# TensorE's instructions tied to the program's order in three stages of an encoder layer, and six more filling steps ahead of the attention's scores

## The chip, the cores and the metric

The kernel runs on one NeuronCore of one Trainium2 chip. The metric is the device time of one execution in microseconds. A core has engines with one in-order instruction stream each: TensorE (PE: matrix products, and transposes as products with an identity; PEld is its loading of the stationary operand), VectorE (DVE), ScalarE (ACT), GpSimd (POOL) and SyncE (SP, which issues most DMAs here). They meet at semaphores.

## What is computed

One layer on a sequence of 1024 tokens of width 1024, all in float32:

```
x = x + 1/2 post1(SwiGLU1(pre1(x)))                       # FFN, 2816 wide
u = pre_mix(x)
q,k,v,g of the retention | q,k,v of the attention | two gates = u @ W_mix_in
y_ret = W_ret_out(silu(g) * headnorm(retention forward + backward))   # 4 heads, chunks of 128
y_na  = W_na_out(neighbourhood attention on a 16 x 64 grid, 8 heads of 64, 8 x 16 window, with a bias)
x = x + post_mix(W_mix_out(sigmoid(gate_ret) * y_ret + sigmoid(gate_na) * y_na))
x = x + 1/2 post2(SwiGLU2(pre2(x)))
```

pre and post are RMS norms.

## The kernel before

**Products.** float32 is carried as a high part and a low part (`Core.split`: ScalarE casts the high part at L60, VectorE subtracts at L61). `Core.mm3` (L85 to L89) makes one product of three TensorE instructions: high by high (L87), high by low (L88), low by high (L89). The big products of the FFNs and of W_mix_in use a Strassen-Winograd scheme (`Winograd`, `Pairs`). PSUM has eight banks: six go round under the name `ps`, two under `pt` (transposes).

**Who sets the order.** The program is traced in the order in which Python emits it, and at the end a planner orders each engine's instructions. It simulates the engines with costs of its own and gives an engine, among the instructions whose inputs are ready in that simulation, the one that was emitted first. So an instruction that isn't ready in the plan is overtaken by later ones that are. The chip then runs each engine's stream strictly in the planned order. It is the planner, too, that hands out the buffers of a tile's name.

**The attention** (`na_cores`, called at L1262). 32 units: 4 pairs of heads, 8 units each. A unit's steps:

- scores (`scores`, L744): two heads, two products of 384 columns each; VectorE adds the bias and finds the maximum (L745), ScalarE takes exp (L749), VectorE the reciprocal (L751) and the scaling (L753). The tile `s` has two buffers.
- `flip` (L763): six transposes into two `pt` banks, split to `pth` and `ptl` by ScalarE and VectorE (L60, L61).
- `values`: nine products of 256 columns, copied to `ot` by ScalarE (L779).

The loop emits, for i: the scores of unit i, `fill(n1)`, the flip of unit i-1, the values of unit i-2, `fill(n2)`. Ahead of the loop it loads the first keys and queries and calls `fill(n0)`. The three numbers are `NA_FILL`.

**Filling.** `Filler` steps a generator, `products` (L1227 on): the retention's v (two projections of 64 steps, the lines of `vproj`, L1121; their banks are copied out at L1139), then the two sigmoid gates (`gate`, L1221 and L1223, 192 steps), then W_na_out (64 steps, L1254 and L1256). A step is one `mm3` of 512 columns. One more step only sets the mark "rv". After the attention, `fill.until("rv")` makes sure that v is done.

**The retention** (`ret_cores`, called at L1266). Four heads of eight chunks: backwards, states from `update` (L922) with `fill` between; then per chunk scores (L936), three products (L1010 to L1013), norms on ScalarE, VectorE and GpSimd (L949 to L957), and `store` with two transposes (L966). `RET_FILL` holds its counts of filling steps. What is left of the generator runs in `fill.drain()` behind it. Then W_ret_out (L1294) reads the result back and splits it into `xy`.

**From W_mix_out's product to the last norm** (L1331 on). `Core.out_proj` works on groups of token tiles (0,1,2), (3,4,5), (6,7), two banks for each tile. `Ep` takes the finished banks of a tile through the post norm (squares L219, scaling L226 that frees the banks, residual L228, squares L230) and `norm_T` through FFN2's pre norm (L117). Its transposes (`Core.flip`, L126) are kept in the list `left` for some products and emitted between them. `Winograd.put` makes FFN2's operands of them. `Pairs.lead` then makes the first two products of four pairs of FFN2, with the last tiles' transposes emitted between; FFN2 (`ffn_in`) follows.

Of the kernel before, what the change touches and what calls it, by code (L numbers as in the profile page):

```python
# [1 line left out]

# [1 line left out]

# [22 lines left out]
RH = 4  # L27
NHP = 4

NA_FILL = (12, 2, 2)  # L30
RET_FILL = (14, 2, 2, 4, 2, 3, 0, 1, 2)
FLIP_FILL = (8, 8, 8, 8, 2)
NA_UNITS = ((0, 0, 0), (3, 1, 0), (1, 0, 1), (1, 0, 2), (4, 1, 1), (4, 1, 2), (2, 0, 3), (5, 1, 3))
# [4 lines left out]
class Core:  # L38
# [97 lines left out]
    def out_proj(self, nk, lhs, wload, done, groups=((0, 1, 2), (3, 4, 5), (6, 7)), tail=3, lag=8, space=3):  # L136

        left = []  # L140

        def one(t, k, a, w):
            for e in [e for e in left if e[0] <= 0]:
                left.remove(e)
                f = e[1]()
                if f is not None:
                    left.append([2, f])
            for b in range(2):
                self.mm3(banks[t][b], a[t], w[b], k == 0, k == nk - 1)
            for e in left:  # L150
                e[0] -= 1

        for toks in groups:
            banks = {t: [self.bank() for _ in range(2)] for t in toks}
            tl = tail if len(toks) > 1 else 0
            for k in range(nk - tl):
                w, a = wload(k), lhs(k, toks)
                for t in toks:
                    one(t, k, a, w)
            last = [(k, lhs(k, toks), wload(k)) for k in range(nk - tl, nk)]  # L160
            for t in toks:
                for k, a, w in last:
                    one(t, k, a, w)
                f = done(t, banks[t])
                if f is not None:
                    left.append([max(lag, max([e[0] for e in left], default=-space) + space), f])
        return [f for _, f in left]


class Filler:  # L170
# [267 lines left out]
class LeftFactors:  # L438


    order = [j + h * FT // 2 for j in range(FT // 2) for h in range(2)]
# [232 lines left out]
def stream(c, pool, src):  # L674

    def lhs(k, toks):
        n = len(toks) * P
        p0 = toks[0] * P
        raw = pool.tile([P, 384], F32, tag="graw", name="graw", bufs=2)
        h = pool.tile([P, 384], F32R, tag="gh", name="gh", bufs=3)  # L680
        l = pool.tile([P, 384], F32R, tag="gl", name="gl", bufs=3)
        c.nc.sync.dma_start(raw[:, :n], src(k)[:, p0:p0 + n])
        c.split(h[:, :n], l[:, :n], raw[:, :n])
        return {t: (h[:, j * P:(j + 1) * P], l[:, j * P:(j + 1) * P]) for j, t in enumerate(toks)}
    return lhs
# [344 lines left out]
def trunk_layer(ctx: ExitStack, tc, x, g1a, w1i, w1o, g1b, gma, wmt, wnv, wrv, logits, dtab, rope, bias,  # L1030
# [7 lines left out]
    c = Core(tc, const, wpool, psum, dram)  # L1038
# [18 lines left out]
    def rows(a):  # L1057
        return lambda t: a[t * P:(t + 1) * P, :]
# [3 lines left out]
    def pool(stack, name, side="left"):  # L1062
        return stack.enter_context(tc.tile_pool(name=name, bufs=1, side=side))
# [28 lines left out]
    ep = pool(ep_stack, "ep1")  # L1092
# [165 lines left out]

    fill = Filler(products())
    dec = []  # L1260
    with tc.tile_pool(name="na", bufs=1) as na:
        na_cores(c, na, d, bias, fill, *NA_FILL, {24: lambda: dec.append(Decays(c, mix, logits, dtab))})  # L1262
    dec = dec[0]
    fill.until("rv")
    with tc.tile_pool(name="ret", bufs=1) as ret:
        ret_cores(c, ret, mix, d, dec, fill, RET_FILL)  # L1266
    y_stack = ExitStack()
    ypool = pool(y_stack, "y")
# [44 lines left out]
    cmb = pool(left, "cmb2")  # L1313
    wx = Winograd(c, (apool,) * 3, cmb, (14,) * 7)
    wx.s3_on_pool = (4, 5)
    with tc.tile_pool(name="ep2", bufs=1) as ep:
        rest = c.out_proj(KT, stream(c, gs, lambda k: d["m"][k]), lambda k: c.load_w(wmo[k]),
                          Ep(c, ep, gmb, g2a, False, rows(x1), rows(x2), wx.put))
        fin = Pairs(c, wx, [(w2i[i], w2i[FT + i]) for i in LeftFactors.order], 3, 1)

        def save():
            return [gs.tile([P, 384], F32, tag=n, name=n, bufs=3)[:, :256] for n in ("gh", "gl")]

        fin.lead(save, rest)
        for f in rest:
            f()
# [94 lines left out]
```

## Time and profile before

| | us |
|---|---|
| median of 3 runs | 2334.3 (2330.53 to 2337.57) |
| the profiled execution | 2332.5 |
| its span, first to last instruction | 2330.7 |
| TensorE busy | 2226.6 (96%) |
| VectorE busy | 1677.0 (72%) |
| ScalarE busy | 1008.0 (43%) |
| GpSimd busy | 598.9 (26%) |

In the chain that ended last TensorE has 84% of the span. The attention takes from about 998 to 1246 us, the retention to 1471, W_ret_out to about 1558, W_mix_out's product and its norms to 1706. In the rows, `out<-in` are the program's tile names, a number behind "L" is a line of the kernel, and "idle before" is the time in which the engine stood still before the instruction, with what ended it. A product's rows overlap: the distance of two starts is what the product costs in a row of them.

### The profile page before, as it was taken

Reading aid. Unit: us, or ns where it says so; the run is one execution under the profiler, and the core shown is the slowest. Engines: PE = TensorE matmul, PEld = TensorE weight load, DVE = VectorE, ACT = ScalarE, POOL = GpSimd, SP = SyncE. Lnnn points to the kernel's source line nnn. Section 1 sums busy time; section 2 is a strip of 40 time slices with the busy share of each in tenths; the row PEclk is TensorE's granted clock in tenths of the full one; section 3 lists DMA queues with packets and bytes.
Section 4 is the critical chain, followed back from the end, with each engine's and each line's share of the span. In section 5 each row is a group of like instructions: output and inputs, shape, how many; then the busy total and the mean of one; then the engine's idle time right before and its main releaser. Section 6 shows DMA issues by size and latency. Waiting matters only on the chain.

```text
span 2330.7 us, 30323 instructions
## 1 busy us (share of the span) xinstructions
PE 2226.6 (96%) x10288; PEld 1849.4 (79%) x10288; DVE 1677.0 (72%) x2939; ACT 1008.0 (43%) x2104; POOL 598.9 (26%) x749
## 2 busy tenths in 40 slices
PE   6999999999998999989889999998889999999998
PEld 5888888778886888877768888887668888887886
DVE  7887777745878588867865678545887778775575
ACT  6332222344553223367765676324633222234453
POOL 3144343300440144311101222101322434431032
PEclk9999999999998999999989999999999999999999
DMA  5355555576753444466634467765524555547674
GB/s 190 109 181 174 197 177 185 199 233 189 257 175 112 168 131 131 137 217 202 195 107 152 161 222 231 263 230 188 194 91 142 197 176 200 181 154 235 190 243 142
DMA packets 161884, 422.64 MB, mean 181 GB/s; under 512 B 19712, under 2 KB 47488, under 8 KB 161664
## 3 DMA queue, kind: packets, MB, share of 16 engines
q1 hardware_dynamic: 121248, 286.97, 38.4%
q0 software_dynamic: 40480, 133.72, 15.6%
q8 instruction: 81, 1.33, 0.2%
q14 instruction: 75, 0.61, 0.1%
HBM read 301.60 MB, written 123.21 MB: 182 GB/s over the span
## 4 chain that ended last, share of the span: by engine, by line
PE 84%; issue 6%; DVE 4%; DMA 2%; ACT 2%; POOL 1%; SPq 0%; POOLq 0%; DVEq 0%; ACTq 0%
PE ps L87 26%; PE ps L88 26%; PE ps L89 26%; PE pt L88 1%; PE pt L89 1%; PE pt L87 1%; DMA graw<-g0a 1%; PE pt L126 1%; DVE tmp L117 0%; DVE wl L61 0%; DMA graw<-m 0%; PE pt L914 0%; DMA kraw<-nk 0%; PE pt L966 0%; DVE gl L61 0%
## 5 line engine op out<-in xcount | busy, mean ns | idle before, releaser
L61 DVE TENSOR_TENSOR wl<-wraw,wh 128x512 fp32r<-128x512 f32 x662 | 460.3, 719 | 97.4 <-ACT wh L60 94.5
L60 ACT CAST wh<-wraw 128x512 fp32r<-128x512 f32 x670 | 391.7, 619 | 277.3 <-PE ps L88 110.0
L87 PE MATMUL ps<-wh,gh 128*128 128x512 f32 x612 | 239.2, 393 | 17.2 <-ACT gh L60 12.8
L88 PE MATMUL ps<-wl,gh 128*128 128x512 f32 x612 | 239.4, 391 | 0.0
L61 DVE TENSOR_TENSOR gl<-graw,gh 128x512 fp32r<-128x512 f32 (+2 forms) x178 | 128.9, 728 | 149.2 <-ACT gh L60 146.0
L89 PE MATMUL ps<-wh,gl 128*128 128x512 f32 x612 | 229.1, 392 | 1.1 <-DVE gl L61 1.1
L60 ACT CAST gh<-graw 128x512 fp32r<-128x512 f32 (+2 forms) x178 | 106.5, 602 | 210.6 <-PE ps L88 72.0
L87 PEld LDWEIGHTS ps<-wh,gh 128*128 128x128 f32 x612 | 115.5, 189 | 44.8 <-ACT gh L60 12.9
L526 POOL TENSOR_TENSOR q<-q,gain 128x512 f32<-128x512 f32 x30 | 58.1, 1958 | 334.4 <-PE ps L88 122.1
L89 PEld LDWEIGHTS ps<-wh,gl 128*128 128x128 f32 x612 | 114.8, 188 | 26.3 <-DVE gl L61 2.8
L88 PEld LDWEIGHTS ps<-wl,gh 128*128 128x128 f32 x612 | 115.5, 189 | 23.7
L60 ACT CAST wh<-t 128x512 fp32r<-128x512 f32 x58 | 36.1, 623 | 192.7 <-DVE t L384 192.6
L87 PE MATMUL ps<-a11h,wh 128*128 128x512 f32 x280 | 113.1, 404 | 1.9 <-DVE tmp L226 1.9
L89 PE MATMUL ps<-a11h,wl 128*128 128x512 f32 x280 | 111.7, 399 | 0.0
L88 PE MATMUL ps<-a11l,wh 128*128 128x512 f32 x280 | 111.4, 398 | 0.0
L87 PE MATMUL ps<-a12h,wh 128*128 128x512 f32 x280 | 110.6, 395 | 0.1
L88 PE MATMUL ps<-a12l,wh 128*128 128x512 f32 x280 | 109.8, 392 | 0.0
L89 PE MATMUL ps<-a12h,wl 128*128 128x512 f32 x280 | 109.6, 391 | 0.0
L87 PE MATMUL ps<-a22h,wh 128*128 128x512 f32 x280 | 109.5, 391 | 0.0
L89 PE MATMUL ps<-a22h,wl 128*128 128x512 f32 x280 | 109.2, 390 | 0.0
L88 PE MATMUL ps<-a22l,wh 128*128 128x512 f32 x280 | 109.1, 389 | 0.0
L400 DVE TENSOR_TENSOR c<-ps,gt 128x512 f32<-128x512 f32 x44 | 30.4, 691 | 107.2 <-PE ps L89 107.1
(362 smaller groups left out, 6006.6 us busy)
## 6 DMA issues: line engine op xcount, KB each, us to landing
wraw<-in_dram SPq DMA_DIRECT2D x243, 512.0 KB, 4.3
lead<-in_dram POOLq DMA_DIRECT2D x44, 256.0 KB, 3.9
g0s<-cmb POOLq DMA_DIRECT2D x44, 256.0 KB, 3.2
graw<-g0s SPq DMA_DIRECT2D x44, 256.0 KB, 2.8
wq<-in_dram POOLq DMA_DIRECT2D x44, 256.0 KB, 3.8
g1s<-cmb POOLq DMA_DIRECT2D x44, 256.0 KB, 2.7
graw<-g1s SPq DMA_DIRECT2D x44, 256.0 KB, 2.7
bt<-in_dram SPq DMA_DIRECT2D x24, 384.0 KB, 3.9
```

Of the source, the lines that this page charges most:

```text
L60: nc.scalar.copy(h, src)
L61: (eng or nc.vector).tensor_tensor(l, src, hf, ALU.subtract)
L87: mm(ps, a[0], b[0], start=start, stop=False, skip_group_check=more)
L88: mm(ps, a[0], b[1], start=False, stop=False, skip_group_check=more)
L89: mm(ps, a[1], b[0], start=False, stop=stop, skip_group_check=more)
L126: self.nc.tensor.transpose(pt[:, j * P:(j + 1) * P], h[:, j * P:(j + 1) * P], self.ident)
L400: self.last = self.read = tt(c21, p7, c12, ALU.add).ins
L526: (eng or c.nc.gpsimd).tensor_tensor(h if out is None else out, h, self.post[:, b * 512:(b + 1) * 512], ALU.mult)
```

## The change

Three `with` statements get a second manager, `in_order(c, mybir.EngineType.PE)`: around the attention, around the retention, and around the part from W_mix_out's product to the last norm and FFN2's first products. When such a block ends, every TensorE instruction traced in it gets an edge to the TensorE instruction traced before it. The edges are of the class `NoSync`: the planner keeps them, and no semaphore is added. Other engines are planned as before. `NA_FILL` goes from (12, 2, 2) to (18, 2, 2). No instruction is added or removed.

```diff
-NA_FILL = (12, 2, 2)
+NA_FILL = (18, 2, 2)
...
+@contextmanager
+def in_order(c, engine):
+
+    traced = c.nc.cur_bb.bb.instructions
+    n = len(traced)
+    yield
+    prev = None
+    for i in c.nc.cur_bb.bb.instructions[n:]:
+        if i.engine == engine:
+            if prev is not None:
+                c.tc.add_manual_dep(i, prev.name, mybir.DependencyInfo(
+                    mybir.DependencyClass.NoSync, mybir.DependencyReason.DATA), reason="order")
+            prev = i
...
-    with tc.tile_pool(name="na", bufs=1) as na:
+    with tc.tile_pool(name="na", bufs=1) as na, in_order(c, mybir.EngineType.PE):
         na_cores(c, na, d, bias, fill, *NA_FILL, {24: lambda: dec.append(Decays(c, mix, logits, dtab))})
...
-    with tc.tile_pool(name="ret", bufs=1) as ret:
+    with tc.tile_pool(name="ret", bufs=1) as ret, in_order(c, mybir.EngineType.PE):
         ret_cores(c, ret, mix, d, dec, fill, RET_FILL)
...
-    with tc.tile_pool(name="ep2", bufs=1) as ep:
+    with tc.tile_pool(name="ep2", bufs=1) as ep, in_order(c, mybir.EngineType.PE):
         rest = c.out_proj(KT, stream(c, gs, lambda k: d["m"][k]), lambda k: c.load_w(wmo[k]),
```

More of the change, by code (lines that the diff above doesn't have):

```diff
@@ L1 @@
-from contextlib import ExitStack
+from contextlib import ExitStack, contextmanager
 import numpy as np
```

## The prediction

> **What bounds the kernel now.** I read the table of busy time by stretch first (engines in the order PE, PEld, DVE, ACT, POOL; then the granted TensorE clock, the DMA share and GB/s).
>
> ```profile
> 998.00:1030.00 32.00, 25.50 (x107) 20.57 (x106) 21.79 (x50) 20.84 (x44) 5.23 (x7) 0.89 0.91 292
> 1030.00:1233.00 203.00, 180.64 (x980) 155.29 (x979) 142.44 (x423) 140.00 (x359) 15.17 (x21) 0.94 0.51 156
> 1233.00:1246.00 13.00, 9.75 (x47) 8.05 (x46) 4.64 (x8) 6.11 (x13) 1.07 (x2) 0.91 0.74 259
> 1246.00:1471.00 225.00, 224.27 (x1289) 195.53 (x1287) 163.90 (x426) 139.90 (x364) 53.87 (x84) 1.00 0.59 191
> 1585.00:1640.00 55.00, 48.70 (x215) 38.67 (x213) 38.34 (x69) 31.46 (x75) 7.07 (x11) 0.97 0.56 183
> 1640.00:1706.00 66.00, 49.62 (x217) 39.05 (x217) 59.32 (x98) 37.49 (x84) 24.00 (x25) 0.94 0.52 177
> ```
>
> The first three rows are the attention, the fourth the retention, the last two the stretch from W_mix_out's product to the last norm. TensorE is idle 6.5, 22.4 and 3.3 us in the attention, 0.7 in the retention, 6.3 and 16.4 behind W_mix_out. So the retention has nothing to win and something to lose, and the attention holds most of what the order can touch. In 1640 to 1706 VectorE is busy 59.32 of 66 us, TensorE 49.62: there the order of TensorE isn't the limit.
>
> Next, the waits of TensorE in the attention's long stretch, 1030 to 1233 (total, times, longest), and one of VectorE's:
>
> ```profile
> PE ps L87 <- ACT pth L60: 14.4, 10, 3.6
> PE ps L88 <- DVE ptl L61: 4.8, 4, 2.5
> PE pt L763 <- DVE ptl L61: 1.6, 3, 0.7
> ...
> DVE s L745 <- PE pt L763: 12.3, 9, 4.0
> ```
>
> 19.2 us of the 22.4 that TensorE is idle there are spent by the product with the values, which waits for the split of transposed probabilities (pth, ptl). The last row says that VectorE stands 12.3 us ahead of the scores' sum with the bias, because its tile s has two buffers and TensorE hasn't transposed the one before last. The timeline of TensorE (start, duration, instruction, idle time before it and who ended it) late in the attention:
>
> ```profile
> 1197.33 0.34 PE L744 MATMUL ps<-k,qh 128*128 128x384 f32 x1
> 1197.51 0.34 PE L744 MATMUL ps<-k,ql 128*128 128x384 f32 x1
> ...
> 1198.73 0.49 PE L763 MATMUL pt<-ident,s 128*128 128x128 f32 x3
> 1198.98 0.36 PE L88 MATMUL ps<-ptl,vh 128*128 128x256 f32 x1
> ...
> 1199.42 0.28 PE L88 MATMUL ps<-ptl,vh 128*128 128x256 f32 x1
> 1199.54 0.28 PE L89 MATMUL ps<-pth,vl 128*128 128x256 f32 x1
> 1202.63 0.54 PE L87 MATMUL ps<-pth,vh 128*128 128x256 f32 x1 [2.81 <-ACT pth L60]
> ...
> 1204.25 0.63 PE L87 MATMUL ps<-a21h,wh 128*128 128x512 f32 x1
> 1204.68 0.63 PE L88 MATMUL ps<-a21l,wh 128*128 128x512 f32 x1
> ...
> 1207.42 0.39 PE L88 MATMUL ps<-a21l,wh 128*128 128x512 f32 x1
> 1207.65 0.39 PE L89 MATMUL ps<-a21h,wl 128*128 128x512 f32 x1
> ```
>
> The planner has put the transposes late and close against the product with the values of the same unit; at 1202.63 the product stands 2.81 us for a split that began just before. The two filling products after it start 0.43 us apart, three microseconds later 0.23: after such a wait the clock is halved for a while. The program's own order puts a whole unit of other work between the two.
>
> **The change, part by part.** Durations are of the profiled execution (2332.5 us, 1.8 under the median of 2334.3).
>
> *The cycle in the order of emission.* Per unit: scores of unit i (4 products at 0.18, 1197.33 to 1197.51), two filling steps (6 at 0.23), six transposes of unit i-1 (some 0.1 each: three from 1198.73, 0.25 to the next product), nine products with the values of i-2 (at 0.12, 1199.42 to 1199.54), two filling steps: 0.7 + 1.4 + 0.6 + 1.1 + 1.4 = 5.2 us. From the transposes of a unit to its values lie 1.1 + 1.4 + 0.7 + 1.4 + 0.6 = 5.2 us of TensorE's work; the split there takes a few tile passes. So the **19.2 us are taken as gone**; bounds 0 and 19.2.
>
> *What is late next.* The transposes stand at the head of TensorE's queue, and behind them the values, the filling and the next scores. Between the scores of a unit and its transposes lie 1.4 + 0.6 + 1.1 + 1.4 + 0.7 + 1.4 = 6.6 us. The chain that has to fit (sum with the bias, exp, reciprocal, scaling) is seen in the timeline of the engines for two units:
>
> ```profile
> 1199.26 0.56 DVE L745 CUSTOM_DVE_ANT_0 s<-ps,bt 128x384 f32<-128x384 f32 x1 [0.98 <-PE pt L763]
> 1204.94 0.75 DVE L753 TENSOR_SCALAR s<-s,ss 128x384 f32<-128x384 f32 x2
> 1210.22 0.56 DVE L745 CUSTOM_DVE_ANT_0 s<-ps,bt 128x384 f32<-128x384 f32 x1 [1.02 <-PE pt L763]
> 1212.85 1.28 ACT L1223 ACT_TABLE_LOAD   x1
> 1217.59 0.75 DVE L753 TENSOR_SCALAR s<-s,ss 128x384 f32<-128x384 f32 x2
> ```
>
> 6.4 us (1199.26 to 1205.69) and 8.1 (1210.22 to 1218.34). Both begin only when the buffer of s is free; strict order transposes earlier, so that wait goes. At 6.4 the new stall is 0, at 8.1 it is 1.5 a unit, for some 31 units 47 us. The second holds a sigmoid between two table loads, which only the end of the stage has. I take 0.3 a unit, **+10**, near the lower end, because VectorE (142.44 of 203) and ScalarE (140.00) have slack.
>
> *The clock.* Granted 0.94 over 203 us is 12.2 us of full-speed work lost at most. Short waits don't cost it, as the quieter middle of the stage shows beside the 2.81 us wait:
>
> ```profile
> 1128.00:1188.00 60.00, 54.05 (x312) 46.30 (x311) 47.08 (x154) 44.49 (x120) 3.78 (x7) 1.00 0.63 196
> 1199.00:1207.00 8.00, 5.19 (x22) 4.43 (x20) 3.87 (x13) 5.66 (x14) 0.00 (x0) 0.79 0.09 35
> ```
>
> 6 us of idling in 60, and the clock stays at 1.00. With stalls of 0.3 a unit I take back **-8** (0 to -12.2). The Trainium skill (TensorE: Matmul & The Clock Gate, "The HAM clock gate") halves the clock only after an idle window of about 3.4 us. By that the wait of 2.81 would have cost nothing, and the trace disagrees: 0.43 us apart behind it. By the rule alone the term would be about -2, for the one wait of 3.6, and the sum 6 us higher.
>
> *Eighteen filling steps ahead of the scores.* 18 x 3 x 0.23 = 12.4 us from 998.46, to 1010.9; the first score product ran here at 1011.15.
>
> ```profile
> 998.46 0.39 PE L87 MATMUL ps<-wh,a11h 128*128 128x512 f32 x1
> ...
> 1011.15 0.34 PE L744 MATMUL ps<-k,qh 128*128 128x384 f32 x1
> ...
> 1017.45 0.44 PE L744 MATMUL ps<-k,qh 128*128 128x384 f32 x1 [1.03 <-DVE nast L745]
> ...
> 1023.01 1.66 PE L763 MATMUL pt<-ident,s 128*128 128x128 f32 x6 [4.40 <-DVE s L753]
> ```
>
> The old planner filled these microseconds without being told, so the six steps replace what it did: 0. The waits at 1017 and 1023 (5.4 us) are the first chain through an empty pipeline and stay. At the other end six steps are missing: 18 + 136 in the attention and 234 in the retention ask for 388 of the 385 that exist (384 of work and one that only marks), where 382 were asked for. In the last microseconds of the retention:
>
> ```profile
> 1467.92 0.51 ACT L957 ACTIVATE yn<-y,rstd 128x256 f32<-128x256 f32 x1 [0.94 <-POOL rstd L97]
> 1470.10 0.38 PE L966 MATMUL pt<-ident,yn 128*128 128x128 f32 x2
> 1470.57 2.94 ACT L60 CAST xy<-wraw 128x1024 fp32r<-128x1024 f32 x3 [2.14 <-PE pt L966]
> ```
>
> The last transposes could start at 1468.43 and start at 1470.10, behind filling; W_ret_out's first split waits for them. Taking 6 x 3 x 0.23 = 4.1 us of filling away lets this end 1.7 us sooner, so **+2.4** (0 to +4.1).
>
> *The change of stage.* The 3.3 us idle in 1233 to 1246 is the wait for the retention's first keys. In strict order 2 + 14 filling steps, 10.9 us, stand behind the last values; **-2** (0 to -3.3).
>
> *Retention in strict order.* Nothing can be gained beyond 0.7. Its cycle in the text of the program has four filling steps (2.7 us) in every chunk between a state's update and its use, and only the first updates stand close behind the transposes that feed them. I take **+3** (0 to +10).
>
> *From W_mix_out to the last norm.* Waits of TensorE in 1585 to 1714:
>
> ```profile
> PE ps L87 <- ACT s2h L60: 6.6, 1, 6.6
> PE ps L87 <- DVE tmp L226: 6.4, 4, 1.9
> PE ps L87 <- ACT gh L60: 5.4, 3, 3.0
> PE pt L126 <- DVE tmp L117: 3.9, 3, 2.2
> ```
>
> The L226 waits are for banks of the tiles before; in strict order the third token tile's first products block two others that now run ahead, which can double them (+6.4). At the end 48 products of FFN2's first factors stand behind the last transposes instead of ahead, 10.9 us that cover the 6.6 behind s2h, but they also delay by what they cover. VectorE's 59.32 of 66 us sets that end in either order: **0** (-8 to +10).
>
> Sum: -19.2 + 10 - 8 - 2 + 3 + 2.4 + 0 = -13.8. 2332.5 - 13.8 = 2318.7, and with the 1.8 to the median **2320.5 us**.
>
> **The rivals.** *The wait only changes its name* (0.25): the chain takes 7.2 us, 0.6 over what lies between, so 19 us of new stalls at the transposes instead of 10, and the clock returns 4 instead of 8: the sum is about -1, 2333. For it: VectorE waited 12.3 us for TensorE, and the planner, which put the transposes late, seems to reckon with a long chain. Against: the 12.3 us come from that lateness itself.
>
> *Slower* (0.18): the chain takes 8.1 us in every unit, as the one that ended at 1218.34. Then 47 us of stalls stand against 19.2, nothing comes back of the clock, and the sum is +31, 2366. It decides from 7.5 us on: 0.9 x 31 = 28, and -19.2 + 28 - 4 - 2 + 5.4 = +8. The Trainium skill's "A second HAM failure mode" on the same page points the same way: frequent small idling between groups of products can make the clock swing. Against it stands the row with 1.00 at 10% idle.
>
> *More* (0.12): the stalls stay near 0, the clock returns whole, and the covered end behind W_mix_out gives 8: -19.2 - 12.2 - 3.3 - 8 + 5.4 = -37, 2297.
>
> *It does nothing in the retention*: the planner's order there may already be the program's; that moves the sum by 3 and is inside the range.
>
> **How the numbers follow.** The forecast has 0.45. Its own range is 2308 to 2331. The range for 8 in 10 reaches down to the large gain and up past no change, not to the end of the slow case: 2298 to 2345. Within 0.3% is 2327.3 to 2341.3, what a measurement of this kernel can hardly tell from none. Faster: 0.43 of the forecast's 0.45, 0.12, and 0.02 of the first rival, 0.57. Same: 0.02, 0.20 and 0.02, 0.24. Slower: 0.03 and 0.16, 0.19.
>
> **What would show it.** Right: the waits for pth and ptl in the attention nearly gone, VectorE's wait for the transposes gone, the clock near 1.00 there, the attention some 17 us shorter, the retention within a few microseconds of 225. Wrong: a row of transposes waiting for s L753 of more than 20 us; a retention with idle TensorE; or banks (L226) holding the stretch behind W_mix_out for 10 us more than before.

## The result, and the profile after

| | us |
|---|---|
| median of 5 runs after | 2312.9 (2309.86 to 2314.31) |
| median of 5 runs before, same chip | 2334.7 (2330.53 to 2337.71) |
| ratio | 0.9904, 95% interval 0.9889 to 0.9919 |
| the profiled execution after | 2313.7 (span 2311.8) |

That is 21.8 us faster between the medians, where 13.8 were forecast. The table of busy time by stretch of the changed kernel (columns as in the prediction):

```profile
998.00:1030.00 32.00, 27.83 (x124) 22.16 (x123) 22.38 (x53) 22.48 (x49) 5.08 (x6) 0.95 0.89 289
1030.00:1209.00 179.00, 165.42 (x941) 144.22 (x940) 140.49 (x421) 132.43 (x348) 15.28 (x21) 0.96 0.56 177
1209.00:1220.00 11.00, 11.00 (x52) 9.05 (x51) 3.72 (x6) 5.76 (x12) 1.07 (x2) 1.00 0.61 205
1220.00:1450.00 230.00, 226.26 (x1308) 197.38 (x1306) 168.57 (x429) 142.59 (x369) 53.51 (x85) 1.00 0.58 194
1450.00:1539.00 89.00, 89.00 (x385) 73.36 (x386) 41.17 (x60) 19.69 (x29) 4.50 (x8) 0.98 0.70 250
...
1538.80:1691.10 152.30, 127.91 (x546) 103.58 (x545) 112.17 (x190) 79.57 (x177) 32.31 (x37) 0.90 0.55 184
1538.80:2088.20 549.40, 525.01 (x2297) 432.51 (x2296) 407.29 (x648) 200.61 (x394) 172.93 (x233) 0.97 0.49 170
```

The rows are the start of the attention, its long stretch, the change of stage, the retention, W_ret_out, W_mix_out to the last norm, and the same with FFN2 up to its own output product. The same cuts of the kernel before, attention and retention in one:

```profile
998.50:1471.70 473.20, 439.70 (x2418) 379.06 (x2416) 333.24 (x908) 307.52 (x780) 75.61 (x114) 0.96 0.58 185
...
1558.50:1705.60 147.10, 124.73 (x547) 99.56 (x545) 109.39 (x186) 77.11 (x175) 31.60 (x37) 0.96 0.57 190
1558.50:2106.50 548.00, 524.53 (x2298) 430.01 (x2297) 407.71 (x648) 200.22 (x393) 172.59 (x232) 0.98 0.50 170
```

Attention and retention went from 473.2 us to 452.0 (998 to 1450). That is the whole gain: W_ret_out takes 2.0 us more (88.8 to W_mix_out's first product at 1538.8, before 86.8 from 1471.7 to 1558.5), W_mix_out to the last norm 5.2 more, of which FFN2 gives 3.8 back. Filling moved between attention and retention, so the two are compared together.

The waits of TensorE in the attention, 998 to 1220, then those of VectorE in its long stretch (total, times, longest):

```profile
PE pt L778 <- DVE s L768: 13.4, 6, 4.0
PE pt L778 <- DVE ptl L61: 1.6, 2, 1.0
PE ps L759 <- ACT qh L63: 1.5, 1, 1.5
...
DVE ss L766 <- ACT s L764: 13.7, 17, 2.4
...
DVE s L760 <- PE ps L759: 4.8, 6, 2.9
...
```

(Lines behind the new function stand 15 higher: L763 is L778, L753 is L768, L744 is L759, L745 is L760, L226 is L241.) The product with the values waits no more; both rows of it are gone (the waits left out are of 0.6 us and less). VectorE's 12.3 us for the transposes are gone too (the rows left out are waits for ScalarE). What is new is 13.4 us of transposes that wait for scaled probabilities, not a little in every unit but in six waits.

### The profile page after: what moved, and what is told of

It is laid out like the page before. It is cut to its first block, busy times and chain, and to the rows that moved or that the text cites. A ratio compares the mean times of both kernels' runs of the same rounds, so it can differ in the third digit from the quotient of the medians.

```text
span 2311.8 us, 30270 instructions
## 1 busy us (share of the span) xinstructions
PE 2218.9 (96%) x10288; PEld 1846.7 (80%) x10288; DVE 1678.4 (73%) x2939; ACT 1004.0 (43%) x2102; POOL 598.1 (26%) x749
## 4 chain that ended last, share of the span: by engine, by line
PE 88%; DVE 5%; ACT 2%; DMA 2%; issue 1%; POOL 0%; SPq 0%; POOLq 0%; DVEq 0%; ACTq 0%
PE ps L87 27%; PE ps L88 27%; PE ps L89 27%; PE pt L88 1%; PE pt L89 1%; PE pt L87 1%; PE pt L126 1%; DVE wl L61 1%; PE pt L778 1%; DMA graw<-g0a 1%; DMA qraw<-nq 1%; DVE s L760 1%; DVE tmp L117 0%; PE ps L759 0%; ACT s L764 0%
## 5 line engine op out<-in xcount | busy, mean ns | idle before, releaser
L89 PE MATMUL ps<-wh,gl 128*128 128x512 f32 x612 | 234.7, 393 | 0.1
```

The costliest lines, as they stand in the source:

```text
L89: mm(ps, a[1], b[0], start=False, stop=stop, skip_group_check=more)
```

## The experiments

All were timed in five rounds, beside the kernel before on the same chip. `in_order` is the function of the change.

| kernel | median us | ratio to before, 95% interval |
|---|---|---|
| fill18: six steps, no order | 2314.0 | 0.9922 (0.9910 to 0.9935) |
| fill24: twelve steps, no order | 2321.9 | 0.9948 (0.9935 to 0.9960) |
| na_only: order in the attention, 12 steps | 2308.7 | 0.9897 (0.9883 to 0.9910) |
| ret_only: order in the retention | 2334.7 | 1.0012 (1.0004 to 1.0021) |
| ep_only: order behind W_mix_out | 2334.6 | 1.0013 (1.0004 to 1.0022) |
| na18: order in the attention, 18 steps | 2307.4 | 0.9888 (0.9873 to 0.9903) |
| na31: na18, three steps behind the scores, one behind the values | 2301.8 | 0.9871 (0.9857 to 0.9884) |
| na18_tail: na18, six steps fewer in the retention (two ahead of it, one a head) | 2302.7 | 0.9871 (0.9857 to 0.9885) |
| changed2: the changed kernel again | 2311.9 | 0.9906 (0.9889 to 0.9924) |
| no_ep: changed, without the order behind W_mix_out | 2309.2 | 0.9899 (0.9882 to 0.9916) |
| na31_tail: na31 and na18_tail together | 2297.0 | 0.9842 (0.9822 to 0.9862) |
| na31_tail_k2: the next keys loaded two units earlier | 2299.4 | 0.9852 (0.9835 to 0.9870) |

### Each part of the change alone

```diff
# fill18, on the kernel before
-NA_FILL = (12, 2, 2)
+NA_FILL = (18, 2, 2)
# na_only, on the kernel before
-    with tc.tile_pool(name="na", bufs=1) as na:
+    with tc.tile_pool(name="na", bufs=1) as na, in_order(c, mybir.EngineType.PE):
# ret_only, on the kernel before
-    with tc.tile_pool(name="ret", bufs=1) as ret:
+    with tc.tile_pool(name="ret", bufs=1) as ret, in_order(c, mybir.EngineType.PE):
# ep_only, on the kernel before
-    with tc.tile_pool(name="ep2", bufs=1) as ep:
+    with tc.tile_pool(name="ep2", bufs=1) as ep, in_order(c, mybir.EngineType.PE):
```

> The kernel before with NA_FILL (18, 2, 2) and no order. Theory A (the order in the attention brings the 22 us, the six steps nothing): 0 to +3 us, because the planner filled the start anyway and the retention's tail lacks six steps. Theory B (the six filling steps cover the first chain and bring most of it): -10 us or more. Theory C (the retention's order brings it): 0.

> The order in the attention alone, NA_FILL (12, 2, 2). Theory A: -16 to -25 us, values' waits for pth and ptl in the attention under 2 us where they were 20. Theory B: -3 to -8. Theory C: within 5 us of before.

> The order in the retention alone. Theory A: -1 to +4 us, since TensorE was idle 0.7 us in 225 there. Theory B: 0. Theory C: -10 us or more.

> The order from W_mix_out's product to the last norm alone. Theory A: 0 to +4 us (the comparison of the two traces shows that stretch 5 us longer and FFN2 behind it 4 us shorter). Theory B and C: 0. If this part carried the gain: -5 us or more.

The order in the attention alone gives 24 us (0.0103 of 2332), as much as the whole change; that is theory A's forecast for it. The two largest waits of TensorE in na_only, 998 to 1210:

```profile
PE pt L778 <- DVE s L768: 17.6, 6, 5.2
PE ps L759 <- issue: 3.5, 1, 3.5
```

No wait for pth or ptl is left: it is the order that removes them. But the six steps alone, without any order, give 18 us, where theory A had 0 to +3 and I had put them at 0. The two don't add: each gives most of the gain without the other. The first 32 us of the attention in fill18, and its waits from 998 to 1210:

```profile
998.00:1030.00 32.00, 30.79 (x143) 25.55 (x142) 22.89 (x50) 22.28 (x47) 5.02 (x6) 1.00 0.93 306
```

```profile
PE ps L87 <- ACT pth L60: 10.8, 11, 2.1
...
PE ps L88 <- DVE ptl L61: 2.5, 3, 1.9
```

In these 32 us TensorE is busy 30.79 where it was 25.50, and its clock is 1.00 where it was 0.89: 5.3 us and, at 0.11 of 32, some 3.5. The wait of 4.40 ahead of the first transposes is gone. So about 9 of the 18 us come from the start, where the planner had not filled all it could. The wait at the change of stage is gone as well (13.00 of 13 us busy, before 9.75), while a wait of 3.40 us for the last norm has come at the end of the retention. The values still wait for the split.

Order in the retention costs 2.8 us (0.9 to 4.9) when it comes alone, order behind W_mix_out 3.0 (0.9 to 5.1). From 1246 to 1475 us TensorE waits a single 1.0 us in the retention of ret_only. But ahead of the retention's first transposes of keys it stands longer. Their rows in the kernel before, then in ret_only:

```profile
1241.53 1.06 PE L914 MATMUL pt<-ident,kraw 128*128 128x128 f32 x8 [1.78 <-issue]
1244.07 1.97 PE L914 MATMUL pt<-ident,kraw 128*128 128x128 f32 x8 [1.47 <-DVE kdl L64]
```

```profile
1244.76 1.09 PE L929 MATMUL pt<-ident,kraw 128*128 128x128 f32 x4 [6.24 <-issue]
```

That is 6.24 us where 3.25 were, 3.0 more, the size of the loss. In ret_only the load of these keys was issued at 1240.6 us, before at 1236.9. Whether the order or the plan of the attention ahead of it made it late isn't decided; the changed kernel has no such wait. The waits of TensorE in ep_only from W_mix_out to FFN2:

```profile
PE pt L126 <- DVE tmp L117: 13.2, 4, 5.0
PE ps L87 <- DVE tmp L241: 10.9, 3, 6.6
```

What the first rival feared for the attention happened here, waits that only change their name: the 6.6 us behind s2h and the 5.4 for gh are gone, and 9 more for transposed tiles (13.2 against 3.9) and 4.5 more for banks (10.9 against 6.4) have come.

### How many steps, with and without order

```diff
# fill24, on the kernel before
-NA_FILL = (12, 2, 2)
+NA_FILL = (24, 2, 2)
# na18, on na_only
-NA_FILL = (12, 2, 2)
+NA_FILL = (18, 2, 2)
```

> NA_FILL (24, 2, 2), no order. Theory D (in the free plan the extra steps help because they put more filling between the first scores and the first transposes): the start stays covered, twelve steps are missing at the tail of the retention, so 2 to 6 us slower than with 18: 2316 to 2320. Theory E (the free plan lands by chance within some 10 us, whatever the number): anything from 2312 to 2335, and the idle time of the steady attention (beyond its first 40 us) differs by more than 5 us from that with 18.

> The order in the attention alone, NA_FILL (18, 2, 2). If the order behind W_mix_out costs what its trace showed (some 6 us) and the order in the retention a little: 2303 to 2308, faster than the changed kernel by 5 us or more. If the three orders need each other: 2311 to 2315. Against the order in the attention with 12 steps: the start 7 us shorter, the tail 3 to 4 longer, so 2 to 5 us in all.

Six steps more on top of fill18 lose 6 us of its 18. The start and the long stretch of fill24:

```profile
998.00:1030.00 32.00, 31.59 (x149) 26.23 (x148) 21.44 (x49) 20.53 (x43) 5.04 (x6) 1.00 0.91 300
1030.00:1215.00 185.00, 164.57 (x900) 144.08 (x899) 137.86 (x418) 135.32 (x350) 14.61 (x21) 0.94 0.54 168
```

Its start is as clean as that of fill18. Its long stretch idles 20.4 us at a clock of 0.94, where fill18 idles 18.1 at 0.97 (166.86 of 185 us busy), and two waits ahead of the retention's first transposes, 1.65 and 1.31 us, are back. So the gain at the start came at both counts, and what fill18 won behind it didn't: without order, the plan of the units came out better or worse with the count. Why better at 18 is open. Theory D's range was missed by 2 us; theory E's holds the time, but its sign, 5 us of difference in the idle time, didn't come.

With the order in the attention the six steps are worth 1.3 us (2308.7 and 2307.4, on different chips, the intervals overlap), less than the 2 to 5 that I expected. At the start they do help: in the first 32 us na_only waits 3.5, 5.2 and 1.3 us, na18 3.5, 1.5 and 0.7, 4.3 less in all. (The changed kernel, whose attention is written as na18's, waits 2.0, 1.5 and 0.7, so single executions differ by 1.5 here.) The end of the retention takes it back, as the next pair shows.

### Where the steps go

```diff
# na31, on na18
-NA_FILL = (18, 2, 2)
+NA_FILL = (18, 3, 1)
# na18_tail, on na18
-RET_FILL = (14, 2, 2, 4, 2, 3, 0, 1, 2)
+RET_FILL = (12, 2, 2, 3, 2, 3, 0, 1, 2)
```

> As na18 with NA_FILL (18, 3, 1): 0.7 us more of TensorE's work between a unit's scores and its transposes, as much less between one unit's turn and the next. If the new stalls at the transposes are a chain that is too long by a little in many units: their idle time falls from 15.6 to 10 us or less and the time by 3 to 6 us. If they are bursts on ScalarE (keys, queries, copies of the filling in front of exp) in a few units: no change beyond 2 us.

> As na18 with RET_FILL (12, 2, 2, 3, 2, 3, 0, 1, 2): six filling steps fewer ahead of and inside the retention, so six more are left for its last two stores. If the missing filling there costs what its trace showed (3.7 us idle and a halved clock behind it): 2.5 to 5 us faster than na18. If the retention needs those steps where they were: no gain, idle time inside the retention.

A step moved from behind the values to behind the scores gives 5.6 us between the medians; the intervals overlap a little. Between the scores of a unit and its transposes the steps behind the scores come twice and those behind the values once: seven steps instead of six, 0.7 us more for the chain. TensorE's waits for it in the attention, in na18 and in na31:

```profile
PE pt L778 <- DVE s L768: 14.8, 6, 4.0
```

```profile
PE pt L778 <- DVE s L768: 7.8, 4, 3.7
```

The time came out as the first theory had it, but the waits are few and long, as the second had them: six, then four. The 0.7 us of room shorten them or take them away.

The steps taken from the retention (two ahead of it, one in each head: six, not the "four a head" of a later expectation) give 4.7 us, again with intervals that overlap. The end of the retention (TensorE) in the changed kernel, in na18, and in na18_tail:

```profile
1448.39 0.44 PE L981 MATMUL pt<-ident,yn 128*128 128x128 f32 x2 [2.57 <-ACT yn L972]
1450.00 2.63 PE L87 MATMUL ps<-xy,wh 128*128 128x512 f32 x6 [1.18 <-ACT xy L60]
```

```profile
1449.11 0.69 PE L981 MATMUL pt<-ident,yn 128*128 128x128 f32 x2 [3.41 <-ACT yn L972]
1450.97 2.93 PE L87 MATMUL ps<-xy,wh 128*128 128x512 f32 x6 [1.18 <-ACT xy L60]
```

```profile
1441.28 0.38 PE L981 MATMUL pt<-ident,yn 128*128 128x128 f32 x2
1442.84 1.66 PE L87 MATMUL ps<-xy,wh 128*128 128x512 f32 x6 [1.18 <-ACT xy L60]
```

With 388 steps asked of 385, the changed kernel has nothing left to put ahead of the last two transposes and stands 2.57 us for their norm; six products of W_ret_out then take 2.63 us instead of 1.66, at half the clock. In na18 the same wait is 3.41 us and the six products take 2.93: 3.41 and 1.27 are the 4.7. In na18_tail filling runs up to the transposes. The 1.18 us ahead of W_ret_out are no part of it: all three have them, and the kernel before has 1.19.

### Together, and against the changed kernel

```diff
# no_ep, on the changed kernel
-    with tc.tile_pool(name="ep2", bufs=1) as ep, in_order(c, mybir.EngineType.PE):
+    with tc.tile_pool(name="ep2", bufs=1) as ep:
# na31_tail, on the kernel before
-NA_FILL = (12, 2, 2)
+NA_FILL = (18, 3, 1)
-RET_FILL = (14, 2, 2, 4, 2, 3, 0, 1, 2)
+RET_FILL = (12, 2, 2, 3, 2, 3, 0, 1, 2)
-    with tc.tile_pool(name="na", bufs=1) as na:
+    with tc.tile_pool(name="na", bufs=1) as na, in_order(c, mybir.EngineType.PE):
```

> The changed kernel unchanged, beside the others on one chip. Its own time was 2312.9 us, 0.9904 of the kernel before; it should repeat within 2 us. It is what the next three are compared with.

> The changed kernel without the order behind W_mix_out; attention and retention keep theirs. Theory that the order there costs: in the changed kernel W_mix_out's product to FFN2's first product took 152.3 us and FFN2 397.1; in the kernels without that order 143 and 400. The difference, 9 less 3, is 6 us: 2306 to 2309 us expected. Rival, that the free plan's own stretch varies with whatever comes ahead of it (147.1 in the kernel before, 143 in others): with these earlier stages it could come out at 147, and the time would be 2311 to 2313.

> Order in the attention alone, 18 filling steps ahead, three behind the scores and one behind the values, and four filling steps a head taken out of the retention's counts. Apart, the steps moved behind the scores gave -5.6 us against the same kernel with two and two, and the steps taken from the retention -4.7. If the gains lie in different places (stalls of transposes; the end of the retention) they add: 2296 to 2300 us. If both are the same few stalls of the attention, which in single profiles ran 4 us apart on the same plan: about 2301.

The changed kernel repeated. Taking the order behind W_mix_out away gave 2.7 us between the medians, but the intervals overlap almost wholly: the 6 us that I expected of it are not shown. In no_ep the waits are back at 6.5 (s2h), 6.3 (L241), 4.5 (transposes) and 3.6 (gh), and the stretch to FFN2's output product is 546.4 us against 549.4, which agrees in sign with ep_only.

The two gains add: na31_tail is 36 us under the kernel before (2297.0 and 2333.2, ratio 0.9842) and 15 under the changed kernel on the same chip. It is the best of all, with one of the three orders.

### The waits that are left

```diff
# na31_tail_k2, on na31_tail
-            if j == 4 and hp + 1 < NHP:
+            if j == 2 and hp + 1 < NHP:
                 load(hp + 1)
```

> The kernel with three and one and the retention's steps taken out, with the next pair of heads' keys and values loaded and cast after the third unit of a pair instead of after the fifth. Theory that the two stalls of the transposes which are left (2.6 and 3.7 us, in the last units of a pair, with the clock halved behind them) come from ScalarE, which makes the keys' casts, the queries and the copies of the filling in one burst ahead of an exp: they shrink to half or less, and the kernel is 3 to 6 us faster than the one without this edit. Theory that the chain from scores to scaled probabilities is as long without the casts: no change, within 2 us.

No change. But the edit moved hardly anything, so the theory wasn't tested. TensorE's last scores of the first pair and ScalarE's casts of new keys, in na31_tail_k2:

```profile
1051.43 0.34 PE L759 MATMUL ps<-k,ql 128*128 128x384 f32 x1
...
1054.38 1.13 ACT L60 CAST k<-kraw 64x512 fp32r<-64x512 f32 x2
```

In na31_tail these stand at 1053.88 and 1056.83: the casts come 2.95 us behind the scores in both. The tiles of keys have two buffers, and the keys of the third pair go where the first pair's lie. So what sets their time isn't where the load stands in the program but the last scores that read the old ones. For the fourth pair the casts come 1.93 us behind the scores in na31_tail and 1.44 in na31_tail_k2, and the wait is 3.67 us (up to 1112.59) and 3.17. A third buffer of the keys was not tried.

What the burst does is seen in the changed kernel. TensorE's wait, and what it is halved to; then ScalarE, VectorE and GpSimd ahead of it:

```profile
1062.98 1.57 PE L778 MATMUL pt<-ident,s 128*128 128x128 f32 x6 [3.67 <-DVE s L768]
...
1066.27 0.63 PE L87 MATMUL ps<-wh,a21h 128*128 128x512 f32 x1
1066.70 0.63 PE L88 MATMUL ps<-wl,a21h 128*128 128x512 f32 x1
...
1055.44 1.14 ACT L60 CAST k<-kraw 64x512 fp32r<-64x512 f32 x2
1056.61 1.07 ACT L1154 COPY ev<-ps 128x512 f32<-128x512 f32 x2
...
1058.97 0.63 ACT L764 ACTIVATE s<-s,nast 128x384 f32<-128x384 f32 x1
...
1055.05 0.16 DVE L762 TENSOR_SCALAR nast<-nast 128x2 f32<-128x2 f32 x1
1055.24 1.78 DVE L61 TENSOR_TENSOR k<-kraw,k 64x512 fp32r<-64x512 f32 x1
1057.05 1.40 DVE L64 SCALAR_TENSOR_TENSOR ql<-qraw,qh 128x256 fp32r<-128x256 f32 x1
1058.48 0.69 DVE L61 TENSOR_TENSOR k<-kraw,k 64x512 fp32r<-64x512 f32 x1
...
1055.19 1.29 POOL L61 TENSOR_TENSOR k<-kraw,k 64x512 fp32r<-64x512 f32 x1 [0.59 <-DVE ql L64]
1056.66 1.50 POOL L61 TENSOR_TENSOR k<-kraw,k 64x512 fp32r<-64x512 f32 x1 [0.18 <-ACT k L60]
```

The maximum of unit 7 was ready at 1055.21 (1055.05 and 0.16), its exp began at 1058.97: ScalarE had casts and copies to do first. The transposes of the unit stood 3.67 us. The longest wait, 4.02 us, is the next of this kind (TensorE, ScalarE, VectorE):

```profile
1113.67 1.57 PE L778 MATMUL pt<-ident,s 128*128 128x128 f32 x6 [4.02 <-DVE s L768]
...
1108.57 0.62 ACT L764 ACTIVATE s<-s,nast 128x384 f32<-128x384 f32 x1 [0.24 <-DVE nast L762]
...
1108.38 0.15 DVE L762 TENSOR_SCALAR nast<-nast 128x2 f32<-128x2 f32 x1
```

Here the exp followed the maximum at once, and it was VectorE that was late: the unit's scores were summed by 1104.98, their maximum was made ready only at 1108.38, behind splits of keys and queries of 1.66 and 1.40 us that overlap GpSimd's (last section). After the exp other splits came first again; the reciprocal ran at 1112.38, 2.5 us behind its end. So the theory of na31_tail_k2, which named ScalarE alone, had only a part of the burst.

## Why the prediction was right, point by point

- *Values' waits, -19.2.* Right: all gone, and na_only shows that the order does it. But the lateness of the transposes was only part of the wait that I quoted. The split for 1202.63 began at 1202.12, 2.9 us behind the transposes, because ScalarE had a table load (1.28 us from 1199.62) and two exps to do first; the wait of 3.63 at 1217.77 has the same ahead of it. The chain that I gave as 6.4 us stood behind these loads too, not only the one of 8.1.
- *New stalls of the transposes, +10.* The size came out right by luck, the place was wrong. Of the 13.4 us, 2.0 are the first chain of the start; 11.4 are new in the long stretch. I spread 0.3 us over every unit, from a mean chain between 6.4 and 8.1. In fact most units wait nothing, and 3.67 and 4.02 us fall on two units, where the buffers of keys come free. The trace of the kernel before had it. From the sum to the end of the scaling its 32 units take 3.6 to 10.1 us, and the longest isn't at a sigmoid but here, where the fourth pair's keys are cast:

```profile
1110.33 0.55 DVE L745 CUSTOM_DVE_ANT_0 s<-ps,bt 128x384 f32<-128x384 f32 x1
...
1119.71 0.75 DVE L753 TENSOR_SCALAR s<-s,ss 128x384 f32<-128x384 f32 x2
```

That rival of 0.25 and the slower one, which put 7.2 or 8.1 us on every unit, fell.
- *Clock, -8.* By the column of the granted clock: before (0.11 x 32, 0.06 x 203, 0.09 x 13) 16.9 us lost, after (0.05 x 32, 0.04 x 179, 0) 8.8. That is -8.1, right in size but partly by luck: only 5.0 of it are in the stretch that it was meant for.
- *Eighteen steps, 0 at the start.* This step was wrong. TensorE idles 4.2 us of the first 32 instead of 6.5, and 1.9 of the clock's 8.1 lie there too; alone the steps gave 9. I held that the planner had filled these microseconds already, and that the first chain's waits would stay at 5.4. They are 2.0 (at 1021.56) and 1.5 (for a query). The rows that I quoted, 1.03 and 4.40 idle, said that there was room.
- *Six steps fewer at the end, +2.4.* Too small: the idle time is 2.57 us, near the forecast, but W_ret_out is 2.0 longer behind the halved clock; na18_tail gives 4.7 for steps put back. I counted the missing filling, not the clock behind it. With the attention in order the six steps give at one end what they take at the other: -1.3 between na_only and na18, where I had +2.4 in sum.
- *Change of stage, -2.* 3.3 us idle became 0.
- *Retention, +3.* All its 3.7 us of idling are the two waits at its end, above, and 1.18 of them were there before: the order itself stalls nothing there. Alone it costs 2.8; ret_only's longer wait for the first keys, 3.0 us, is of that size.
- *W_mix_out to the last norm, 0.* +5.2 in the stretch and -3.8 in FFN2, +1.4; ep_only has +3.0 (0.9 to 5.1). The cover of the s2h wait came as described, and so did its price. I named the bank waits; the larger part is the transposes.
- *What would show it.* The retention at 225 us and the attention 17 shorter were read wrongly: they are 230 and 26 shorter, since the order moved filling from one to the other. Only their sum, 21.2, means something.

The long stretch idles 13.6 us where the two first terms gave 13.2. With that (+0.4), the start's idling (-2.3), the change (-1.3), the retention (-3), the end (2.6 idle and 2.0 of clock instead of 2.4, +2.2), W_mix_out (+1.4) and the clock (-0.1), -13.8 becomes -16.5, where the two profiled executions differ by 18.8. The rest is no more than the rounding of the clock's column (0.005 of 473 us is 2.4). The 3 us from there to the 21.8 of the medians are the spread of single executions: the profiled one of changed2 took 2308.4.

The mechanism stated first, that the order trades the values' waits for smaller ones of the transposes, is shown. Not shown is that all three orders are needed: the one in the attention carries the gain, and the other two together with it cost up to 4 us (0.9904 and 0.9906 against na18's 0.9888, with overlapping intervals).

## What to carry to other kernels

Where a planner works with its own costs, a software pipeline written by hand is worth pinning on the bound engine only where its waits show that the plan undoes it; here one stage of three. Try the counts of filling alone before the pin: they gave 18 of the 22 us without it, though not in a way that held at the next count. When filling is moved to the front of a stage, look at the end of the generator, and price a gap there with the clock behind it.

## What the runs showed of the hardware

**The length of a wait doesn't tell whether the clock is halved behind it.** Two waits of TensorE in the changed kernel, 1.45 us up to 1012.21 and 1.59 us up to 1098.64, and the table of busy time just behind each:

```profile
1012.21 0.44 PE L759 MATMUL ps<-k,qh 128*128 128x384 f32 x1 [1.45 <-ACT qh L63]
...
1098.64 1.25 PE L778 MATMUL pt<-ident,s 128*128 128x128 f32 x6 [1.59 <-DVE s L768]
```

```profile
1013.47:1016.88 3.41, 3.41 (x10) 2.64 (x9) 3.15 (x9) 2.21 (x5) 0.37 (x1) 0.50 1.02 418
1098.60:1102.00 3.40, 3.33 (x21) 2.78 (x22) 3.37 (x10) 2.95 (x8) 0.00 (x0) 1.00 0.18 24
```

Behind the shorter the clock is 0.50 for 3.41 us, beginning over a microsecond after the wait; behind the longer it is 1.00. What decides between them isn't shown. I had taken short waits as free. The Trainium skill (TensorE: Matmul & The Clock Gate, "The HAM clock gate") tells of a window of about 3.4 us that runs freely, and of an idle one as what halves the clock. The length agrees with the 3.41; that the whole window must be idle doesn't, since 1.45 us was enough.

**VectorE stands while GpSimd splits.** In the rows of 1055 to 1059 the same split takes VectorE 1.78 us beside GpSimd's and 0.69 behind it. It begins 0.05 behind GpSimd's first and ends 0.54 after that one's end (1056.48); the next, 1.40 us, ends 0.29 after the end of GpSimd's second (1058.16). The Trainium skill (SBUF — State Buffer, "Who interferes with whom") says that a VectorE instruction with two inputs in SBUF contends with a GpSimd instruction that reads there, and that the later one blocks for the whole of the earlier; the rows agree. No kernel here gave these splits to another engine, so what it would save isn't known.
